# A hybrid attention block on one core: the FFN's gate and up products as seven block products from block 3 on, and p's projection ahead of the FFN

## Chip, core and metric

The kernel runs on one core of one Trainium2 chip. Such a core has five instruction streams that run beside each other and meet at semaphores: PE (TensorE, matrix products into the eight PSUM banks), DVE (VectorE, elementwise), ACT (ScalarE, activations and copies), POOL (GpSimd) and SP (SyncE, which here only issues transfers). Sixteen DMA engines move data between DRAM and the on-chip memory SBUF. The metric is the device time of one execution in microseconds (us).

## What is computed

One residual block on 512 tokens of width 1024, in float32. The attention part is left out here, since the change leaves its arithmetic as it is.

```python
def conv_ffn(h, w_gate, w_up, conv_w, conv_b, w_down):
    g = h @ w_gate                       # 1024 -> 2816
    gp = jnp.pad(g, ((0, 0), (2, 0), (0, 0)))
    conv = conv_b
    for j in range(3):                   # causal, along the tokens
        conv = conv + gp[:, j:j + s, :] * conv_w[j]
    return (jax.nn.silu(conv) * (h @ w_up)) @ w_down

x = x + concat[mla(h), diff(h)] @ w_out                  # h = rms_norm(x)
x = x + conv_ffn(rms_norm(x, ffn_norm_g), w_gate, w_up, conv_w, conv_b, w_down)
x = x + sigmoid(rms_norm(x, ple_norm_g) @ w_ple_gate) * (p @ w_ple_proj)
```

## The kernel before

Everything is kept transposed: x^T is eight blocks of 128 features by 512 tokens. A float32 product is made of three products of rounded parts: every operand is split into a rounded `hi` (ACT, a copy) and a remainder `lo` (DVE, a subtraction), and `mm3` (L151) issues hi·hi, hi·lo and lo·hi for each 128-row step of the contraction (L154, L155, L156). So a weight tile costs a load on SP's queue into one of three `raw` buffers (`load_w`, L142), an ACT copy (L147) and a DVE subtraction (L148) before PE may use it.

The FFN has 22 blocks of 128 hidden columns. For block f, `gu_full` (L782) makes the gate g and the up u, each 8 steps of the contraction times 3 matmuls of 128x128 by 512 tokens: 48 matmuls. `gu_post` (L768) then multiplies g by the tokens' norm factor r (`nr`; gr, DVE L772), runs the three-tap convolution (ACT L773, DVE L774 and L775), silu (ACT L776), r again (POOL L777), times u (DVE L778), and splits the result into `ah`, `al`. The norm factor is applied after the product, so that the products need only the unnormalised, split x (`h2h`, `h2l`, L191 and L192); r itself is made meanwhile, from one 512-column matmul with ones (L750).

The down projection goes in groups of 6, 6, 6 and 4 blocks: `down` (L794) makes for one of the eight blocks of x^T the sum over the group's blocks, and `add_x` (L575) adds it to x^T from PSUM. A further part, `ple` (L849), closes the kernel: for each block of x^T 24 matmuls for the gate `pg` and 6 for the projection of p (`pp`), then r (L862), sigmoid, times pp (L864), plus x (L865), and a store. It needs the squares of the final x^T summed over its blocks (L744, L745).

PE's order is the order of the code (`manual_schedule` is set for it alone); the order on the other engines is made by a scheduler when the program is built, and each engine, and each DMA queue, then works in that order strictly.

Of the kernel before, what the change touches and what calls it, by code (L numbers as in the profile page):

```python
# [20 lines left out]
P = 128  # L21
# [14 lines left out]
# columns of the packed per-partition array  # L36
# [15 lines left out]
DOWN_GROUPS = (6, 6, 6, 4)  # L52
# [3 lines left out]
# units of filling work at the attention's steps  # L56
# [7 lines left out]
# which of VectorE (0) and GpSimdE (1) does a step, by tiles  # L64
# [35 lines left out]
def hybrid_block(ctx: ExitStack, tc: tile.TileContext, a: dict, out: bass.AP):  # L100
# [4 lines left out]
    sb = ctx.enter_context(tc.tile_pool(name="sb", bufs=1))  # L105
    sm = ctx.enter_context(tc.tile_pool(name="sm", bufs=2))
    pp_ = ctx.enter_context(tc.tile_pool(name="ps", bufs=1, space=PS))
# [5 lines left out]
    def tt(name, dtype=F32):  # L113
        return sb.tile([P, T], dtype, tag="tt", bufs=16, name=name)

    def sq_tile(name):
        return sb.tile([P, D], F32, tag="sq", bufs=2, name=name)

    def pm_tile(name):
        return sb.tile([P, T], F32, tag="pm", bufs=PM, name=name)  # L120

    def pt_tile(name):
        return sb.tile([P, T], F32, tag="pt", bufs=2, name=name)

    def xn_tile(name):
        return sb.tile([P, D], F32, tag="xn", bufs=4, name=name)

    def kv_tile(name, dtype=F32):
        return sb.tile([P, NT, H, 160], dtype, tag="kv", name=name)

    def th_tile(name):
        return sb.tile([P, T], F32R, tag="th", bufs=8, name=name), sb.tile([P, T], F32R, tag="tl", bufs=8, name=name + "l")

    def small(name, shape):
        return sb.tile(shape, F32, name=name)

    def load_raw(src, n, name):
        raw = sb.tile([P, 1024], F32, tag="raw", bufs=3, name=f"raw_{name}")
# [3 lines left out]
    def load_w(src, n, name, eng=None):  # L142
        """a tile of weights as hi + lo"""
        raw = load_raw(src, n, name)
        hi = sb.tile([P, 1024], F32R, tag="hi", bufs=NW, name=f"hi_{name}")
        lo = sb.tile([P, 1024], F32R, tag="lo", bufs=NW, name=f"lo_{name}")
# [4 lines left out]
    def mm3(ps, blocks, first=True, last=True):  # L151
        n = len(blocks)
        for i, (xh, xl, wh, wl) in enumerate(blocks):
            TE.matmul(ps, xh, wh, start=first and i == 0, stop=False)  # L154
            TE.matmul(ps, xh, wl, start=False, stop=False)  # L155
            TE.matmul(ps, xl, wh, start=False, stop=last and i == n - 1)  # L156
# [28 lines left out]
    def split(h_, l_, src, col=None, eng=None):  # L185
        """hi and lo of src, times a gain for each partition"""
# [9 lines left out]
    # the tensor engine's clock and the activation tables get ready while the first loads run  # L196
    ones, warm = small("ones", [P, P]), small("warm", [P, 1])
# [11 lines left out]
    def squares(kq):  # L209
        """squares of x, for the sums over its columns"""  # L210
# [7 lines left out]
    cols = small("cols", [P, NCOL])  # L218
    nc.sync.dma_start(cols, a["cols"])
    xh, xl, wa = [], [], []  # L220
    for kq in range(4):
        raw = xn_tile(f"xT{kq}")
        xraw.append(raw)
        wr = sb.tile([P, 1024], F32, tag="raw", bufs=3, name=f"raw_a{kq}")
        wh, wl = (sb.tile([P, 1024], F32R, tag=i, bufs=NW, name=f"{i}_a{kq}") for i in ("hi", "lo"))
# [21 lines left out]
    ident = small("ident", [P, P])  # L247
# [20 lines left out]
    # latents: normalise  # L268
# [681 lines left out]
```

## Time and profile before

| | us |
|---|---|
| three runs | 702.42, 705.51, 705.87 |
| median | 705.51 |
| span of the profiled execution | 706.7 |
| attention and output projection, to the first FFN matmul | 265.8 |
| PE busy | 677.1 |
| DVE, ACT, POOL busy | 424.2, 288.4, 139.0 |

The span is that of one profiled execution, from the first to the last instruction; it stands 1.2 us above the median of the runs. PE's busy time counts a matmul from its issue to its modelled end, and matmuls overlap in the array, so the distance between two issues, not a matmul's duration, is what one costs. In a timeline row the numbers are start and duration, and in brackets the idle time before it with what ended it. In a row of a group, a count, the busy time, the mean duration in ns, and the idle time before with its releaser. In a row of DMA issues, the last number is the time from issue to landing.

### The profile page before, as it was taken

How to read it: one execution, taken by the hardware profiler on the slowest of the kernel's cores; microseconds unless marked ns; L12 is line 12 of the kernel's file. 1: busy time of each engine (PE TensorE's matmuls, PEld its weight loads, DVE VectorE, ACT ScalarE, POOL GpSimd, SP SyncE). 2: the span in 40 equal slices, each digit the busy share in tenths (PEclk: the TensorE clock that was granted, in tenths of full speed). 3: DMA queues.
4: the chain of work that ended last, by engine and by line, in shares of the span. 5: the costliest groups of instructions: out<-in, count | busy, mean ns of one | idle time of the engine just before them, and what ended most of it. 6: DMA issues, size and time to landing. Idle time of an engine off the chain costs nothing.

```text
span 706.7 us, 8596 instructions
## 1 busy us (share of the span) xinstructions
PE 677.1 (96%) x3242; PEld 554.8 (79%) x3242; DVE 424.2 (60%) x754; ACT 288.4 (41%) x500; POOL 139.0 (20%) x136
## 2 busy tenths in 40 slices
PE   7988889999999997999999999999999999999997
PEld 6877678788878785788888888888888888877886
DVE  6689964634779878774544545534554455468743
ACT  6156645536666654343421333312333233255210
POOL 6458341504010125021100011100101000132000
PEclk9899999999999998999999999999999999999999
DMA  7332014303311103233213333222233132243101
GB/s 261 106 121 89 30 60 135 120 1 111 129 30 61 31 31 105 74 99 110 90 42 108 119 102 106 90 90 89 90 103 103 63 119 90 89 150 104 60 31 45
DMA packets 19552, 63.38 MB, mean 90 GB/s; under 512 B 2220, under 2 KB 2988, under 8 KB 19384
## 3 DMA queue, kind: packets, MB, share of 16 engines
q1 hardware_dynamic: 18776, 60.25, 25.9%
q0 software_dynamic: 448, 2.37, 1.1%
q8 instruction: 25, 0.41, 0.2%
q10 hardware_dynamic: 288, 0.23, 0.1%
q14 instruction: 15, 0.12, 0.1%
HBM read 60.73 MB, written 3.42 MB: 91 GB/s over the span
## 4 chain that ended last, share of the span: by engine, by line
PE 76%; DVE 14%; ACT 3%; issue 2%; POOL 2%; DMA 2%; SPq 0%; ACTq 0%; DVEq 0%; POOLq 0%
PE u L154 6%; PE u L156 6%; PE u L155 6%; PE g L156 6%; PE g L155 6%; PE g L154 6%; PE dn L154 5%; PE dn L155 5%; PE dn L156 5%; PE pg L154 2%; PE pg L156 2%; PE pg L155 2%; PE mo L527 2%; PE zd L154 2%; PE zd L156 2%
## 5 line engine op out<-in xcount | busy, mean ns | idle before, releaser
L777 POOL TENSOR_TENSOR cv<-cv,nr 128x512 f32<-128x512 f32 x22 | 28.7, 1308 | 297.9 <-ACT cv L776 297.9
L155 PE MATMUL g<-h2l,hi_g 128*128 128x512 f32 x176 | 69.6, 396 | 4.7 <-DVE h2l L192 4.7
L154 PE MATMUL dn<-ah,hi_dn 128*128 128x512 f32 x176 | 69.8, 397 | 2.1 <-DVE x L575 2.1
L154 PE MATMUL u<-h2h,hi_u 128*128 128x512 f32 x176 | 70.5, 401 | 0.0
L154 PE MATMUL g<-h2h,hi_g 128*128 128x512 f32 x176 | 70.4, 400 | 0.0
L156 PE MATMUL u<-h2h,lo_u 128*128 128x512 f32 x176 | 70.2, 399 | 0.0
L156 PE MATMUL g<-h2h,lo_g 128*128 128x512 f32 x176 | 70.0, 398 | 0.0
L155 PE MATMUL u<-h2l,hi_u 128*128 128x512 f32 x176 | 69.6, 396 | 0.0
L156 PE MATMUL dn<-ah,lo_dn 128*128 128x512 f32 x176 | 69.5, 395 | 0.0
L575 DVE TENSOR_TENSOR x<-x,dn 128x512 f32<-128x512 f32 x32 | 21.9, 685 | 51.1 <-PE dn L156 51.1
L147 ACT CAST hi_dn<-raw_dn 128x1024 fp32r<-128x1024 f32 x22 | 23.1, 1051 | 69.3 <-PE dn L155 29.7
L772 DVE TENSOR_TENSOR gr<-g,nr 128x512 f32<-128x512 f32 x22 | 15.1, 691 | 53.7 <-PE g L156 53.6
L147 ACT CAST hi_g<-raw_g 128x1024 fp32r<-128x1024 f32 x22 | 23.0, 1047 | 57.9 <-PE dn L155 39.9
L147 ACT CAST hi_u<-raw_u 128x1024 fp32r<-128x1024 f32 x22 | 23.1, 1052 | 55.4 <-PE g L155 50.0
L155 PEld LDWEIGHTS g<-h2l,hi_g 128*128 128x128 f32 x176 | 33.3, 189 | 13.9 <-DVE h2l L192 5.9
L778 DVE TENSOR_TENSOR cv<-cv,u 128x512 f32<-128x512 f32 x22 | 15.1, 688 | 44.4 <-POOL cv L777 44.4
L154 PEld LDWEIGHTS dn<-ah,hi_dn 128*128 128x128 f32 x176 | 33.0, 187 | 10.8 <-DVE x L575 1.9
L154 PE MATMUL zd<-hi_d,xh 128*128 128x512 f32 x96 | 40.2, 418 | 0.0
L156 PEld LDWEIGHTS u<-h2h,lo_u 128*128 128x128 f32 x176 | 33.5, 190 | 8.4
L155 PEld LDWEIGHTS u<-h2l,hi_u 128*128 128x128 f32 x176 | 33.5, 190 | 8.2
L156 PEld LDWEIGHTS g<-h2h,lo_g 128*128 128x128 f32 x176 | 33.3, 189 | 8.1
L154 PEld LDWEIGHTS u<-h2h,hi_u 128*128 128x128 f32 x176 | 33.6, 191 | 7.7
(371 smaller groups left out, 1657.4 us busy)
## 6 DMA issues: line engine op xcount, KB each, us to landing
raw_g<-in_w_gate SPq DMA_DIRECT2D x22, 512.0 KB, 3.6
raw_u<-in_w_up SPq DMA_DIRECT2D x22, 512.0 KB, 3.5
raw_dn<-in_w_down SPq DMA_DIRECT2D x22, 512.0 KB, 3.5
raw_d<-in_w_d SPq DMA_DIRECT2D x12, 512.0 KB, 3.7
raw_o<-in_w_out SPq DMA_DIRECT2D x8, 512.0 KB, 4.0
raw_pg<-in_w_pg SPq DMA_DIRECT2D x8, 512.0 KB, 3.6
x<-in_xT SPq DMA_DIRECT2D x4, 512.0 KB, 5.6
out<-ot SPq DMA_DIRECT2D x7, 256.0 KB, 2.0
```

The lines of the kernel that those rows point to most:

```text
L147: S.copy(hi[:, :n], raw[:, :n])
L154: TE.matmul(ps, xh, wh, start=first and i == 0, stop=False)
L155: TE.matmul(ps, xh, wl, start=False, stop=False)
L156: TE.matmul(ps, xl, wh, start=False, stop=last and i == n - 1)
L527: TE.matmul(po[:, w], pt[:, tsl[j]], kv[j][:, h, 96:], start=j == 0, stop=j == t)
L575: V.tensor_tensor(xb(b), xb(b), ps, op=ALU.add)
L772: V.tensor_tensor(gr, pg_, nrm["r"], op=ALU.mult)
L777: G.tensor_tensor(cv, cv, nrm["r"], op=ALU.mult)
L778: V.tensor_tensor(cv, cv, pu, op=ALU.mult)
```

## The change

**The FFN's products.** From block 3 on (`NPLAIN = 3`), g and u of a block are not two separate products. With the contraction cut into two halves (rows k 0 to 3 and k 4 to 7), the tokens into two halves of 256 columns, and gate and up as the two column blocks of one 2x2 block matrix, a 2x2 by 2x2 block product is made with seven block products and sums (Winograd's form of Strassen's scheme). Each product is 4 steps times 3 matmuls of 256 token columns: 84 matmuls of 256 columns in place of 48 of 512. Products share PSUM: ACT copies a partial sum from one bank to another (L892, L897, L903), and later products are added on top of it (`again`). The seven are named `11`, `12`, `S2`, `S4`, `S3`, `S1` and `22`; two blocks are interleaved on PE: S2(f), 11(f+1), S4(f), S3(f), 12(f+1), S1(f), a down unit, 22(f), a down unit.

**Sums of weights.** One array `w_gu` holds gate and up of a block (1,280 KB with the second copy of a part). An accumulating DMA of 512 KB on POOL's queue (L824) adds gate parts to up parts in SBUF, after the load; two DVE additions (L827, L828) make the other sums `s24`; then four splits follow for each block (`wA`, `wT`, `wS` of 1024 columns, `w22` of 512), of which only `wA` and the raw tile have two buffers.

**Sums of tokens.** The FFN's input is normalised ahead (`tokens`, then `token_sums` for the sums), so r is needed before the first FFN matmul, and gu_post no longer multiplies by r. r itself is now made from four one-column matmuls, a reciprocal square root on 128x4 values, a diagonal matrix `dg` and one matmul `nrb` that spreads it over the partitions.

**The rest.** The projection of p is made ahead of the FFN (`pp_unit`), stored to DRAM (`pps`) and read back in the tail. The down groups are 4, 4, 4, 4, 4 and 2, as units that are called up one at a time. SBUF pools are released and taken anew between stages.

```diff
-DOWN_GROUPS = (6, 6, 6, 4)
+DOWN_GROUPS = (4, 4, 4, 4, 4, 2)
+NPLAIN = 3
...
+    def pp_unit(b):
+        ps, w = bank("acc", f"pp{b}"), wpp[b // 4]
+        mm3(ps, [(w[0][:, c[k]], w[1][:, c[k]], ptw[0][:, k * T:k * T + T], ptw[1][:, k * T:k * T + T]) for k in range(2)])
+        o = pm_tile("ppo")
+        S.copy(o, ps)
+        nc.sync.dma_start(pps[b], o)
...
+    for i, b in enumerate(order):
+        square(i, b)
+    for b in range(NK):
+        pp_unit(b)
+        if b == 1:
+            norm_r()
+        if b == 3:
+            norm_b()
...
+    def raw5(f, n):
+        raw = ffn.tile([P, 2560], F32, tag="raw5", bufs=2, name=f"gu{f}")
+        nc.sync.dma_start(raw[:, :n], a["w_gu"][f][:, :n])
+        return raw
+
+    raws = {0: raw5(0, 2048), 1: raw5(1, 2048)}
...
+    def w_prep(f):
+        raw = raws.pop(f)
+        q = [raw[:, 512 * i:512 * i + 512] for i in range(5)]
+        nc.gpsimd.dma_start(raw[:, 1536:].rearrange("p (i c) -> p i c", i=2), a["w_gu"][f][:, :2048].rearrange("p (i c) -> p i c", i=2)[:, :, :512], accum_op=ALU.add)
+        s24 = ffn.tile([P, 1024], F32, tag="s24", name=f"s24_{f}")
+        wa_ = hl(raw[:, :1024], "wA", f, bufs=2)
+        V.tensor_tensor(s24[:, :512], q[0], q[4], op=ALU.add)
+        V.tensor_tensor(s24[:, 512:], q[1], s24[:, :512], op=ALU.add)
+        wt_ = hl(s24, "wT", f)
+        ws_ = hl(raw[:, 1536:], "wS", f)
+        w2_ = hl(q[2], "w22", f, 512)
+        if f + 2 < NF:
+            raws[f + 2] = raw5(f + 2, 2560)
...
+    def gu_units(f, w):
+        x, g = bank("acc", f"gx{f}")[:, :H2], bank("tp", f"g{f}")
+        product(x, w["11"], tb["11"])
+        S.copy(g[:, t1], x)
+        yield
+        product(g[:, t1], w["12"], tb["21"], True)
+        yield
+        product(x, w["S2"], tb[2], True)
+        S.copy(g[:, t2], x)
+        yield
+        product(g[:, t2], w["S4"], tb["22"], True)
+        yield
+        u = bank("ob", f"u{f}")
+        product(x, w["S3"], tb[3], True)
+        S.copy(u[:, t1], x)
+        yield
+        y = bank("lg", f"gy{f}")[:, :H2]
+        product(y, w["S1"], tb[1])
+        ys = ffn.tile([P, H2], F32, tag="y", name=f"y{f}")
+        S.copy(ys, y)
+        V.tensor_tensor(g[:, t2], g[:, t2], ys, op=ALU.add)
+        V.tensor_tensor(u[:, t2], x, ys, op=ALU.add)
+        yield
+        product(u[:, t1], w["22"], tb[4], True)
+        gu_post(f, g, u, -1.0)
+        yield
...
-        V.tensor_tensor(gr, pg_, nrm["r"], op=ALU.mult)
-        S.activation(cv, gr, AF.Identity, bias=cols[:, C_CB + f:C_CB + f + 1], scale=cw[2])
+        S.activation(cv, g, AF.Identity, bias=cols[:, C_CB + f:C_CB + f + 1], scale=cw[2])
...
-        G.tensor_tensor(cv, cv, nrm["r"], op=ALU.mult)
-        V.tensor_tensor(cv, cv, pu, op=ALU.mult)
+        V.scalar_tensor_tensor(cv, u, sign, cv, op0=ALU.mult, op1=ALU.mult)
...
+    for f in range(NPLAIN, NF):
+        if f + 1 < NF:
+            W[f + 1] = w_prep(f + 1)
+            g1 = gu_units(f + 1, W[f + 1])
+        next(g)
+        if g1:
+            next(g1)
+        next(g)
+        next(g)
+        if g1:
+            next(g1)
+        next(g)
+        pump()
+        next(g)
+        pump()
+        g = g1
```

**Three places in the order of the instructions.** First DVE in the middle of the FFN. Before, for blocks 9 to 12 (`gr` and `cv` belong to gu_post of one block, `lo_g` and `lo_u` are the weights of the block two or three further on):

```order
L772 TENSOR_TENSOR gr_3811<-g9_3761,nr_2928 128x512
L148 TENSOR_TENSOR lo_u11_3908<-raw_u11_3905,hi_u11_3907 128x1024
L774 SCALAR_TENSOR_TENSOR cv_3812<-gr_3811,cols_89,cv_3812 128x511
L775 SCALAR_TENSOR_TENSOR cv_3812<-gr_3811,cols_89,cv_3812 128x510
L778 TENSOR_TENSOR cv_3812<-cv_3812,u9_3762 128x512
L148 TENSOR_TENSOR lo_g12_3977<-raw_g12_3974,hi_g12_3976 128x1024
```

Now, for block 10 on PE, with what each row waits for; `gx10` is the bank x of `gu_units(10)`, `y10` its S1 product, and DMASW is POOL's queue:

```order
L195 TENSOR_TENSOR wTl11_4420<-s24_11_4412,wTh11_4419 128x1024 [waits PE_49,Activation_49]
L195 TENSOR_TENSOR wAl12_4581<-gu12_4276,wAh12_4580 128x1024 [waits DMAHW2_49,Activation_49]
L827 TENSOR_TENSOR s24_12_4579<-gu12_4276 128x512 [waits DMASW4_49,DVE_49]
L828 TENSOR_TENSOR s24_12_4579<-gu12_4276,s24_12_4579 128x512 [waits DVE_49]
L195 TENSOR_TENSOR wSl11_4424<-gu11_4109,wSh11_4423 128x1024 [waits PE_49,Activation_49]
L909 TENSOR_TENSOR g10_4292<-g10_4292,y10_4512 128x256 [waits Activation_49]
L910 TENSOR_TENSOR u10_4473<-gx10_4291,y10_4512 128x256
L581 TENSOR_TENSOR x2_1859<-x2_1859,dn44_4528 128x512 [waits PE_49]
L921 SCALAR_TENSOR_TENSOR cv_4554<-g10_4292,cols_95,cv_4554 128x511 [waits Activation_49]
L922 SCALAR_TENSOR_TENSOR cv_4554<-g10_4292,cols_95,cv_4554 128x510 [waits DVE_49]
L195 TENSOR_TENSOR w22l11_4428<-gu11_4109,w22h11_4427 128x512 [waits PE_49,Activation_49]
```

The sums for block 12, which wait for the accumulating DMA of block 12, now stand ahead of the last weights of block 11 and of the two additions that finish block 10.

Second, SP's queue around the start of the FFN. Before, after the last weights of the output projection:

```order
L139 DMA raw_o13_2720<-in_w_out 128x1024
L139 DMA raw_g0_2864<-in_w_gate 128x1024
L139 DMA raw_u0_2870<-in_w_up 128x1024
L139 DMA raw_g1_2953<-in_w_gate 128x1024
L139 DMA raw_u1_2959<-in_w_up 128x1024
```

Now:

```order
L145 DMA raw_o13_2726<-in_w_out 128x1024
L145 DMA raw_pT_2732<-in_pT 128x1024
L145 DMA raw_pp0_2801<-in_w_pp 128x1024
L145 DMA raw_pp1_2827<-in_w_pp 128x1024
L753 DMA pps_2847<-ppo_2879 128x512
L753 DMA pps_2847<-ppo_2889 128x512
...
L753 DMA pps_2847<-ppo_2962 128x512
L753 DMA pps_2847<-ppo_2972 128x512
L803 DMA gu0_2983<-in_w_gu 128x2048
L803 DMA gu1_2985<-in_w_gu 128x2048
```

The first FFN weights now stand behind the eight stores of p's projection (four of them left out here).

Third, DVE in the tail, at the last down group. Before (`dn18` is the last group, of four blocks, `lo_pg` weights of the last part, `h3l` the split of the finished x^T):

```order
L148 TENSOR_TENSOR lo_dn1811_5224<-raw_dn1811_5221,hi_dn1811_5223 128x1024
L575 TENSOR_TENSOR x3_1855<-x3_1855,dn127_5096 128x512
L575 TENSOR_TENSOR x0_1849<-x0_1849,dn180_5140 128x512
L192 SCALAR_TENSOR_TENSOR h3l_5127<-x0_1849,cols_89,h3h_5126 128x512
L575 TENSOR_TENSOR x0_1849<-x0_1849,dn181_5158 128x512
L148 TENSOR_TENSOR lo_pg00_5326<-raw_pg00_5323,hi_pg00_5325 128x1024
L192 SCALAR_TENSOR_TENSOR h3l_5127<-x0_1849,cols_89,h3h_5126 128x512
L575 TENSOR_TENSOR x1_1851<-x1_1851,dn182_5177 128x512
```

Now (`dn20` is the last group, of two blocks):

```order
L195 TENSOR_TENSOR lo_pg10_6371<-raw_pg10_6368,hi_pg10_6370 128x1024
L581 TENSOR_TENSOR x3_1861<-x3_1861,dn166_6330 128x512
L195 TENSOR_TENSOR lo_pg20_6377<-raw_pg20_6374,hi_pg20_6376 128x1024
L581 TENSOR_TENSOR x3_1861<-x3_1861,dn167_6344 128x512
L195 TENSOR_TENSOR lo_pg30_6383<-raw_pg30_6380,hi_pg30_6382 128x1024
L154 TENSOR_TENSOR lo_dn2000_6394<-raw_dn2000_6391,hi_dn2000_6393 128x1024
L154 TENSOR_TENSOR lo_dn2010_6450<-raw_dn2010_6447,hi_dn2010_6449 128x1024
L581 TENSOR_TENSOR x0_1855<-x0_1855,dn200_6397 128x512
L581 TENSOR_TENSOR x0_1855<-x0_1855,dn201_6408 128x512
L195 TENSOR_TENSOR lo_pg01_6668<-raw_pg01_6665,hi_pg01_6667 128x1024
L198 SCALAR_TENSOR_TENSOR h3l_6387<-x0_1855,cols_95,h3h_6386 128x512 x2
```

The last group's weights now come behind weights of the last part, and a group's product on PE is half as long beside the same DVE work for each block of x^T.

More of the change, by code (lines that the diff above doesn't have):

```diff
@@ L744, in norm_in @@
             S.activation(sq, xb(b), AF.Square)
-            (G if b % 2 else V).tensor_tensor(nrm["ss"], nrm["ss"], sq, op=ALU.add)
+            V.tensor_tensor(nrm["ss"], nrm["ss"], sq, op=ALU.add)
     def norm_r():
-        ps = bank("ob", "nr")
-        TE.matmul(ps, ones, nrm["ss"], start=True, stop=True)
-        r, m, g, t = (w_[:, i] for w_ in [sb.tile([P, DH, T], F32, tag="strip", name="nr")] for i in range(4))
-        rms(r, ps, T, D, m, (g, t))
-        return r
-    h2h = sb.tile([P, NK, T], F32R, tag="st", name="h2h")
@@ L757, in hybrid_block @@
[L757 to L770 removed]
+        ss, ps = nrm["ss"], bank("ob", "nr")
@@ new lines, in product @@
+    def product(ps, w, b, more=False):
+        mm3(ps, [(w[0][:, tsl_k[k]], w[1][:, tsl_k[k]], b[0][:, k], b[1][:, k]) for k in range(K2)], not more, True, more)
+    def gu_units(f, w):
[24 more added lines that the diff above has]
+        yield
@@ L831, in hybrid_block @@
-    h3h = sb.tile([P, NK, T], F32R, tag="st", name="h3h")
-    h3l = kv_tile("h3l", F32R).rearrange("p t h d -> p (t h d)")[:, :NK * T].rearrange("p (k t) -> p k t", t=T)
+    for k in range(NK):
+        tokens(k % K2, k // K2)
+    W[1] = w_plain(1)
+    for k in range(K2):
+        token_sums(k)
+    for f in range(NPLAIN):
+        if f:
+            W[f + 1] = w_plain(f + 1) if f + 1 < NPLAIN else w_prep(f + 1)
+        plain(f, W[f])
+    g = gu_units(NPLAIN, W[NPLAIN])
+    next(g)
+    next(g)
```

288 lines of the change are left out of this document (181 added, 107 removed).

## The prediction

> **What bounds the kernel now.** I read the page's busy times and its chain of waits first, then the windows of the FFN, then single matmuls in the timeline.
>
> ```profile
> PE 677.1 (96%) x3242; PEld 554.8 (79%) x3242; DVE 424.2 (60%) x754; ACT 288.4 (41%) x500; POOL 139.0 (20%) x136
> PE 76%; DVE 14%; ACT 3%; issue 2%; POOL 2%; DMA 2%; SPq 0%; ACTq 0%; DVEq 0%; POOLq 0%
> 300.00:400.00 100.00, 100.00 (x431) 80.64 (x430) 50.79 (x62) 33.06 (x41) 10.61 (x8) 1.00 0.31 95
> 692.97 0.40 PE L156 MATMUL pg<-h3h,lo_pg 128*128 128x512 f32 x1
> 693.20 0.39 PE L154 MATMUL pg<-h3h,hi_pg 128*128 128x512 f32 x1
> 695.28 0.28 PE L154 MATMUL pg<-h3h,hi_pg 128*128 128x256 f32 x1
> ...
> 697.88 0.28 PE L155 MATMUL pg<-h3l,hi_pg 128*128 128x256 f32 x1
> 698.00 0.28 PE L156 MATMUL pg<-h3h,lo_pg 128*128 128x256 f32 x1
> ```
>
> The window row (length, then PE, PEld, DVE, ACT, POOL busy, granted clock, DMA share, GB/s) shows that the FFN is bound by PE alone: busy for all of 100 us at full clock, with DVE at half. 431 matmuls in 100 us are 0.232 us for one of 512 columns, and the first pair of timeline rows has that distance. The three rows after them are the first and the last of 24 matmuls of 256 columns: (698.00 - 695.28) / 23 = 0.118 us for one. A block costs 48 matmuls for gate and up and, spread out, 24 of the down projection: 72 x 0.232 = 16.7 us. So fewer columns on PE do pay, for as long as nothing else takes more than a block's PE time.
>
> **The change, part by part.**
>
> *Products.* In 19 blocks 48 x 0.232 = 11.14 us become 84 x 0.118 = 9.91: 1.23 us each, **-23.5 us** in all. p's projection is 48 matmuls in either place (11.1 us): 0. PE's own time for a block is then 9.9 + 24 x 0.232 = 15.5 us.
>
> *Entry of the FFN.* Before:
>
> ```profile
> 265.76 0.40 PE L154 MATMUL g<-h2h,hi_g 128*128 128x512 f32 x1
> 272.49 0.51 PE L155 MATMUL g<-h2l,hi_g 128*128 128x512 f32 x1 [2.85 <-DVE h2l L192]
> 275.27 0.80 PE L155 MATMUL g<-h2l,hi_g 128*128 128x512 f32 x1 [1.82 <-DVE h2l L192]
> 276.29 0.63 PE L154 MATMUL g<-h2h,hi_g 128*128 128x512 f32 x1
> 276.71 0.63 PE L155 MATMUL g<-h2l,hi_g 128*128 128x512 f32 x1
> 284.91 0.59 PE L750 MATMUL nr<-ss,ones 128*128 128x512 f32 x1
> 274.00:278.00 4.00, 2.73 (x7) 2.03 (x8) 4.00 (x4) 1.86 (x3) 2.32 (x2) 0.57 0.34 131
> L744 ACT ACTIVATE nsq<-x 128x512 f32<-128x512 f32 x7 | 4.3, 615 | 0.0
> L745 DVE TENSOR_TENSOR ss<-ss,nsq 128x512 f32<-128x512 f32 x3 | 2.1, 686 | 0.0
> L188 ACT CAST ah<-cv 128x512 fp32r<-128x512 f32 x22 | 13.7, 621 | 2.4 <-DVE cv L778 2.4
> 250.01 0.17 DVE L161 TENSOR_SCALAR ro<-mo 128x4 int32<-128x4 int32 x1
> ...
> 250.61 0.16 DVE L173 SCALAR_TENSOR_TENSOR ro<-rs_t,ro 128x4 f32<-128x4 f32 x1
> 250.69 0.15 DVE L175 SCALAR_TENSOR_TENSOR rs_g<-rs_t,rs_g 128x4 f32<-128x4 f32 x1
> ...
> 251.55 0.16 DVE L173 SCALAR_TENSOR_TENSOR ro<-rs_t,ro 128x4 f32<-128x4 f32 x1
> raw_g<-in_w_gate SPq DMA_DIRECT2D x22, 512.0 KB, 3.6
> L659 SPq DMA_DIRECT2D x<-in_xT x4: 378/438/510, 171.8 to 173.3; - x4
> DMA to landing us min/median/max: 4.4/5.6/7.2
> 107.43 0.77 POOL L546 DMA_DIRECT2D vec<-vb  x1 [0.30 <-POOL vb L545]
> 109.81 0.58 POOL L547 DMA_DIRECT2D vec<-vec  x1 [1.61 <-DMA vec<-vb]
> vec<-vb POOLq DMA_DIRECT2D x1, 10.0 KB, 2.1
> L147 ACT CAST hi_dn<-raw_dn 128x1024 fp32r<-128x1024 f32 x22 | 23.1, 1051 | 69.3 <-PE dn L155 29.7
> 278.62 1.21 DVE L148 TENSOR_TENSOR lo_u<-raw_u,hi_u 128x1024 fp32r<-128x1024 f32 x1
> ```
>
> Block 0's 48 matmuls ran from 265.76 to 284.91, 19.15 us for 11.14 us of work: 8.0 lost, to waits for h2l and, after them, to a clock of 0.57 (matmuls 0.42 apart). The change has p's projection to fill the first wait, but puts r ahead of everything. The sum of squares has six blocks still to go when PE is done with the output projection: 0.69 + 0.62 + 6 x 0.69 = 5.4 us, against two units of p (2.8): 3 lost. The square root on 128x4 values takes 251.71 - 250.01 = 1.7; with the diagonal (0.69), four small matmuls, the spreading one (0.59 to its end) and some 1.9 for hand-overs and the mean, an estimate, 4.9 us against the next two units' 2.8: 2 lost. Then the second place of the order: gu0's load stands on SP behind the eighth store, which waits for the copy after the last unit. From there a copy (0.62), an issue (0.33) and a load of 1,024 KB. Four loads of 512 KB issued together landed, first to last, (173.3 + 7.2 - 171.8 - 4.4) / 3 = 1.43 us apart, so the load takes 3.5 + 1.43 = 4.95; 0.3 to wake the waiter (issue 107.43, landing 2.1 later, the next instruction at 109.81), hi 1.05, lo 1.2: 8.3 us idle. The stalls bring the half clock back, 13 matmuls x 0.2 = 2.6, and more for three stalls than for two: 4. Together 17.5 against 8.0: **+9.5 us**, between 6 (no clock loss) and 14 (r's steps as slow as the DVE operations beside POOL, below).
>
> *The loop.* The first place of the order closes a ring: the load of gu(f+2) needs the buffer that w22l(f) reads last, and w22 has one buffer, which PE's 22(f-1) must have read. The accumulating DMA waits for that load; s24(f+2) waits for it on DVE; behind s24(f+2) in DVE's order stand wSl(f+1) and the two additions of block f; 22(f) on PE needs the second of them; w22l(f+1) needs 22(f); and the load of gu(f+3) needs w22l(f+1). Once round is one block. Its parts:
>
> ```profile
> L575 DVE TENSOR_TENSOR x<-x,dn 128x512 f32<-128x512 f32 x32 | 21.9, 685 | 51.1 <-PE dn L156 51.1
> L148 DVE TENSOR_TENSOR lo_dn<-raw_dn,hi_dn 128x1024 fp32r<-128x1024 f32 x22 | 27.7, 1261 | 7.0 <-ACT hi_dn L147 6.0
> 698.32 0.42 DVE L862 TENSOR_TENSOR sg<-pg,nr 128x256 f32<-128x256 f32 x1 [1.35 <-PE pg L156]
> strip<-vec POOLq DMA_DIRECT2D x1, 1024.0 KB, 5.4
> 276.40 2.29 DVE L148 TENSOR_TENSOR lo_g<-raw_g,hi_g 128x1024 fp32r<-128x1024 f32 x1
> ```
>
> DVE: two sums of 512 columns (0.69 each), wSl (1.26), two additions of 256 (0.42 each): 3.5. PE: 22, 12 x 0.118 and 0.16 to the end of the last, 1.57. Then w22's hi on ACT 0.62 and lo on DVE 0.69. That is 6.4, and five hand-overs between engines about 0.9. The load of 1,280 KB: 3.5 + 1.5 x 1.43 = 5.65. The accumulating DMA of 512 KB is not in the trace. Below: as a plain one on POOL's queue, 2.1 + (5.4 - 2.1) / 2 = 3.75. Above: its bytes moved twice, as it reads what it writes, 5.4 like the 1,024 KB of strip. I take 4.7, nearer the upper, since every element is read, added and written back. Round: 6.4 + 0.9 + 5.65 + 4.7 = **17.65 us**, from 16.7 to 18.35, where PE needs 15.5. Nothing covers the rest: POOL and SP have no work queued that could start earlier, and PE's next unit is behind 22(f).
>
> By the Trainium skill ("DMA: Bandwidth & Descriptors", section "Anatomy of one DMA — SWDGE (gpsimd) path"), a transfer takes about 2.0 us plus its bytes at 436 GB/s, which gives 3.2 for the 512 KB and 5.0 for the load; the ring would then be 15.5, no longer than PE. The strip row speaks against it: by that fit it would be 4.4, and it took 5.4.
>
> In 14 steady blocks that is 14 x 2.15 = 30 us; laid out from the entry, block 3 (no down units yet to cover anything) loses 5.5, the next two 3, the last ones 1.2: **+40 us**, from 24.5 to 51 with the bounds of the accumulate. Of this some 10 us would stay even with instant transfers: after S1, PE's cover is one down unit (2.8), while hi and lo of wS and the two additions take 3.2, 0.4 in each block, and the start-up remains.
>
> *Tail.* The third place. The last group has two blocks, six matmuls for each block of x^T (1.4 us) where there were twelve (2.8), beside the same DVE work:
>
> ```profile
> L192 DVE SCALAR_TENSOR_TENSOR h3l<-x,cols,h3h 128x512 fp32r<-128x512 f32 x8 | 7.0, 880 | 5.9 <-ACT h3h L191 5.9
> 263.94 0.74 DVE L192 SCALAR_TENSOR_TENSOR h2l<-x,cols,h2h 128x512 fp32r<-128x512 f32 x1
> L148 DVE TENSOR_TENSOR lo_pg<-raw_pg,hi_pg 128x1024 fp32r<-128x1024 f32 x8 | 12.3, 1536 | 1.2 <-ACT hi_pg L147 1.1
> ```
>
> dn2000 is the fifth weight load through three raw buffers, loaded and split behind four of pg: PE waits about 3.2, and 0.9 for the last weights of the group ahead. Then DVE has eight additions (5.5), eight h3l (5.9 undisturbed at 0.74), seven sums of squares (4.8), the lo of dn2010 and of four pg tiles (6.3): 22 us, while PE has the group's 11.1 and a first unit of pg, 5.6, before it needs the last h3l, 16.7. 5.1 more: **+9.5 us** with 0.3 of hand-overs, between 4 (the DVE work that isn't needed for h3l slips back) and 12.
>
> *Small parts.* gu_post loses gr on DVE and the product on POOL, both off PE's path. The normalised tokens and their sums, about 40 us of DVE and ACT over the first blocks, lie beside plain blocks of 11.1 us; their weights are early, so I count 0 for them, and 3 if they are late.
>
> **Sum**: 706.7 - 23.5 + 9.5 + 40 + 9.5 = 742.2, less the 1.2 by which the profiled span exceeds the median of the runs: 741. Forecast **740 us**; with the bounds of its parts 725 to 754.
>
> **Rivals.**
> (a) *The accumulate and the load land so early that the ring is below PE's time.* The loop then keeps the 10 us of start-up and 0.4 per block: 742.2 - 30 - 1.2 = **711**. For it: the DMA share is only 0.31, so nothing competes. Against it: 6.4 us of the ring are durations of this trace, and a plain load of 512 KB alone takes 3.6, of which the ring has one longer and one that is also added.
> (b) *The other side: PE alone paces the kernel.* Without POOL's work beside it DVE is quicker (lo 1.21 alone, 2.29 beside POOL), consecutive DVE operations overlap by some 0.08 at their ends, and if the two hand-overs of the ring fall below 15.5 as well, the loop's waits vanish (1 left) and the tail's shrink to 4: 706.7 - 23.5 + 9.5 + 1 + 4 - 1.2 = **697**. It decides from a ring under 15.5, that is 2.15 us less than my parts; entry must still be paid.
> (c) *The accumulate is slower than its bytes twice*, or PE's idle spells in the loop lower the clock as the 1.8 and 2.9 us did at the entry (0.57). Each us in the ring is 14 + 1.5 = 15.5 us; landing in 6.5 instead of 4.7, the time is 741 + 28 = **769**. For it: 2.1 us waits come in every block, close to the 1.82 that left the clock low. By the Trainium skill ("TensorE: Matmul & The Clock Gate", section "Part 1: The HAM clock gate (the "warmup" mystery)") the clock falls for want of work in a whole window of a few us; no spell here is that long in my sum, and the row at 276.29 stands behind two spells, so I leave it out of the sum.
>
> **How the numbers follow.** Forecast 0.50, (a) 0.17, (b) 0.18, (c) 0.15. A measurement of this kernel tells 0.5%, 3.5 us, from no change. Faster by that (under 702): (b) and 0.02 of (a), 0.20. Within it: 0.05 of (a) and a few of (b)'s upper side: 0.07. Slower: 0.73. The range leaves out half of (b) and two thirds of (c), 0.19: 697 to 766; the likeliest case's own is 725 to 754.
>
> **What would show it.** In the loop's windows: PE's matmuls at 0.118 and 0.232, 108 of them in 17.7 us and not 15.5; the row of 22 waiting about 2 us on DVE's L910 in each block, and L827 waiting for POOL's DMA; the accumulate 4.7 us from issue to landing, the load of gu 5.7. At the entry an idle of some 8 us before the first g matmul, released by DVE's lo of gu0; in the tail, idle before L154 of dn20 and of pg. Wrong is the sum if L827 finds its transfer landed (then 711 or less), if PE idles in a block elsewhere than before 22, or if the clock in the loop is under 0.95. Each term is read by itself: products, entry, loop, tail.

## The result: slower by a tenth, 772 us

| | before | after |
|---|---|---|
| median, us (6 runs each) | 705.01 (702.42 to 706.62) | 772.19 (770.21 to 778.44) |
| span of the profiled execution, us | 706.7 | 776.6 |

The ratio is 1.0975, with a 95% interval from 1.0932 to 1.1018. The profiled execution of the changed kernel was the longest of its six, about 6 us above their median, so the sums below are made against its span of 776.6.

The page of the changed kernel, against the lines shown of before: busy times, granted clock, the chain of waits, and the issues of the block's weights.

```profile
PE 684.1 (88%) x3936; PEld 594.8 (77%) x3936; DVE 493.0 (63%) x909; ACT 348.6 (45%) x629; POOL 104.7 (13%) x117
PEclk8899999999999988989999998999899999999999
PE 36%; DMA 29%; DVE 23%; issue 6%; ACT 4%; POOL 2%; SPq 0%; POOLq 0%; DVEq 0%; ACTq 0%
DMA gu<-in_w_gu 27%; DVE wSl L195 3%; PE u L160 2%; PE pg L160 2%; PE mo L533 2%; PE pg L162 2%; PE pg L161 2%; PE zd L160 2%; PE zd L162 2%; PE zd L161 2%; DVE s L827 2%; PE u L161 2%; DVE w22l L195 2%; PE o L160 1%; PE o L161 1%
gu<-in_w_gu SPq DMA_DIRECT2D x19, 1280.0 KB, 5.6
gu<-in_w_gu POOLq DMA_DIRECT2D x19, 512.0 KB, 6.0
```

PE's busy time even rose, since a matmul's modelled end overlaps the next and there are more of them; the chain tells more. PE had 76% of it and has 36%; DMA had 2% and has 29%, nearly all of it the two transfers of a block's weights. In the wait table of the same execution (who waited for whom, us in total, times, longest) one row holds most of PE's idle time in the FFN:

```profile
PE u L160 <- DVE u L910: 49.9, 18, 6.6
PE g L160 <- ACT wAh L194: 7.4, 1, 7.4
PE dn L160 <- DVE x L581: 3.6, 2, 1.8
PE dn L160 <- ACT hi_dn L153: 3.3, 1, 3.3
PE nr L768 <- DVE ss L762: 3.0, 1, 3.0
```

The first row is the product 22 of each block waiting for the addition u = x + y on DVE. The others are the entry (`wAh` of block 0, `nr`) and the tail (`x`, `hi_dn`). How a block goes round shows in the timeline, here from block 12's 22 to block 13's; the bracket gives the idle time before the row and what ended it:

```profile
516.64 0.69 DVE L827 TENSOR_TENSOR s<-gu 128x512 f32<-128x512 f32 x1 [4.14 <-DMA gu<-in_w_gu]
519.45 0.42 DVE L910 TENSOR_TENSOR u<-gx,y 128x256 f32<-128x256 f32 x1
520.02 0.36 PE L160 MATMUL u<-bth,w22h 128*128 128x256 f32 x1 [3.82 <-DVE u L910]
520.93 0.41 PE L160 MATMUL u<-bth,w22h 128*128 128x256 f32 x1
521.99 0.41 PE L162 MATMUL u<-bth,w22l 128*128 128x256 f32 x1
522.29 0.62 ACT L194 CAST w22h<-gu 128x512 fp32r<-128x512 f32 x1 [1.94 <-PE u L161]
522.94 0.69 DVE L195 TENSOR_TENSOR w22l<-gu,w22h 128x512 fp32r<-128x512 f32 x1 [1.02 <-ACT w22h L194]
523.66 0.33 SPq L803 DMA_DIRECT2D gu<-in_w_gu  x1
529.85 1.20 POOL L824 DMA_DIRECT2D gu<-in_w_gu  x1 [18.82 <-DMA gu<-in_w_gu]
535.97 0.69 DVE L827 TENSOR_TENSOR s<-gu 128x512 f32<-128x512 f32 x1 [2.31 <-DMA gu<-in_w_gu]
539.35 0.35 PE L160 MATMUL u<-bth,w22h 128*128 128x256 f32 x1 [1.99 <-DVE u L910]
```

This is the ring of the prediction, whose links release one another in this order: the sums of weights on DVE, the additions, 22 on PE, the split of the next w22, the next load, the accumulating transfer, the next sums. From L827 to L827 it takes 535.97 - 516.64 = 19.33 us. Over the steady part, 14 rounds from 380.44 to 656.07, the mean is 19.69:

```profile
380.44 0.35 PE L160 MATMUL u<-bth,w22h 128*128 128x256 f32 x1 [3.49 <-DVE u L910]
656.07 0.36 PE L160 MATMUL u<-bth,w22h 128*128 128x256 f32 x1 [2.73 <-DVE u L910]
```

### The profile page after: what moved, and what is told of

Read it like the earlier page. It is cut to its first block, busy times and chain, and to the rows that moved or that the text cites. A ratio compares the mean times of both kernels' runs of the same rounds, so it can differ in the third digit from the quotient of the medians.

```text
span 776.6 us, 10308 instructions
## 1 busy us (share of the span) xinstructions
PE 684.1 (88%) x3936; PEld 594.8 (77%) x3936; DVE 493.0 (63%) x909; ACT 348.6 (45%) x629; POOL 104.7 (13%) x117
## 4 chain that ended last, share of the span: by engine, by line
PE 36%; DMA 29%; DVE 23%; issue 6%; ACT 4%; POOL 2%; SPq 0%; POOLq 0%; DVEq 0%; ACTq 0%
DMA gu<-in_w_gu 27%; DVE wSl L195 3%; PE u L160 2%; PE pg L160 2%; PE mo L533 2%; PE pg L162 2%; PE pg L161 2%; PE zd L160 2%; PE zd L162 2%; PE zd L161 2%; DVE s L827 2%; PE u L161 2%; DVE w22l L195 2%; PE o L160 1%; PE o L161 1%
## 5 line engine op out<-in xcount | busy, mean ns | idle before, releaser
L824 POOL DMA_DIRECT2D gu<-in_w_gu x19 | 22.7, 1194 | 420.4 <-DMA gu<-in_w_gu 304.3
L161 PE MATMUL dn<-al,hi_dn 128*128 128x512 f32 x176 | 73.4, 417 | 0.0
L160 PE MATMUL u<-bth,w22h 128*128 128x256 f32 x76 | 27.2, 358 | 49.9 <-DVE u L910 49.9
L195 DVE TENSOR_TENSOR wTl<-s,wTh 128x1024 fp32r<-128x1024 f32 x19 | 23.3, 1225 | 56.2 <-ACT wTh L194 56.2
L827 DVE TENSOR_TENSOR s<-gu 128x512 f32<-128x512 f32 x19 | 13.2, 692 | 54.3 <-DMA gu<-in_w_gu 52.0
L162 PEld LDWEIGHTS dn<-ah,lo_dn 128*128 128x128 f32 x176 | 35.9, 204 | 10.5 <-DVE lo_dn L154 2.4
L161 PEld LDWEIGHTS dn<-al,hi_dn 128*128 128x128 f32 x176 | 36.5, 207 | 6.6
L161 PE MATMUL zd<-lo_d,xh 128*128 128x512 f32 x96 | 38.3, 399 | 0.0
L521 DVE TENSOR_REDUCE nm<-ml 128x1 f32<-128x128 f32 (+3 forms) x32 | 15.6, 488 | 31.0 <-PE ml L519 31.0
L154 DVE TENSOR_TENSOR lo_dn<-raw_dn,hi_dn 128x1024 fp32r<-128x1024 f32 x22 | 26.8, 1222 | 7.2 <-ACT hi_dn L153 7.2
L195 DVE TENSOR_TENSOR wAl<-gu,wAh 128x1024 fp32r<-128x1024 f32 x22 | 26.8, 1219 | 2.7 <-ACT wAh L194 2.7
L195 DVE TENSOR_TENSOR wSl<-gu,wSh 128x1024 fp32r<-128x1024 f32 x21 | 25.6, 1218 | 3.1 <-ACT wSh L194 3.1
L194 ACT CAST wAh<-gu 128x1024 fp32r<-128x1024 f32 x22 | 23.0, 1044 | 8.9 <-PE g L161 4.5
```

The source lines that it names most:

```text
L154: (eng or V).tensor_tensor(lo[:, :n], raw[:, :n], _f32(hi[:, :n]), op=ALU.subtract)
L160: TE.matmul(ps, xh, wh, start=first and i == 0, stop=False, skip_group_check=again)
L161: TE.matmul(ps, xh, wl, start=False, stop=False, skip_group_check=again)
L162: TE.matmul(ps, xl, wh, start=False, stop=last and i == n - 1, skip_group_check=again)
L194: S.copy(h_, src)
L195: (eng or V).tensor_tensor(l_, src, _f32(h_), op=ALU.subtract)
```

## Experiments

Each shows its edit against the kernel it was built on; unless said otherwise that is the changed kernel. The times of 1 to 7 are of one run each; the kernel before took 706.82 us beside 1 to 4, 708.35 beside 5, and from 702.0 to 708.5 in nine runs beside 6 to 9, so a difference of 4 or 5 us between two single runs is not told by the time alone.

**1. A second buffer for w22.**

```diff
-        w2_ = hl(q[2], "w22", f, 512)
+        w2_ = hl(q[2], "w22", f, 512, 2)
-    t5 = lambda name: ffn.tile([P, T], F32, tag="t5", bufs=3, name=name)
+    t5 = lambda name: ffn.tile([P, T], F32, tag="t5", bufs=1, name=name)
```

> Two buffers for w22 in place of one (and one for cv in place of three, which makes the room). Theory, the ring: the load of gu(f+2) no longer waits for PE's 22 of the block before, only for wSl, and the ring shrinks from the 19.7 us measured between two starts of 22 (DVE 3.4, PE 2.3, ACT and DVE 1.4, load 6.2, accumulate 6.1) to DVE 2.5 + load 6.2 + accumulate 6.1 = 14.8, below PE's 15.5. Blocks then come every 15.5 to 16.5 us, the granted clock in the loop rises above 0.97, and the time falls from 772 by 14 x 3.2 to 14 x 4.2, to 713 to 727. Rival, PE is slowed in the loop by something else than the ring (PSUM traffic of ACT and DVE, or DVE's amount of work): blocks still come every 18 us or more, time above 750.

Measured 730.77 us, 41 less than the changed kernel and 4 above the range. The loop does nearly what was expected, with both transfers still in it: the windows below give 16.6 us for a block (15.5 to 16.5 expected), and the clock is back at 1.00. Some rounds still wait up to 2.8 us for L910. The rival falls.

**2. The same bytes copied, not added.**

```diff
-        nc.gpsimd.dma_start(raw[:, 1536:]..., accum_op=ALU.add)
+        nc.gpsimd.dma_start(raw[:, 1536:]...)
```

> The transfer on POOL's queue copies its 512 KB in place of adding them (the sums of gate and up parts are left out, so the weights are not those of the scheme). Theory, adding costs because every byte is also read back: landing falls from 6.0 us to the 3.75 us that the plain transfers of the kernel before bound it by, the ring from 19.7 to about 17.5, time 772 - 31 = 741 (735 to 748). Rival, the price is that of the software queue (1.2 us of POOL for each issue, descriptors of 2 KB) and not of the adding: landing stays above 5.3 and the time above 760.

Measured 740.23 us. The transfer landed after 4.1 us in place of 6.0 and the round took 17.4 us in place of 19.7. The rival, a landing that stays above 5.3 us, falls. What the edit took away cost 1.9 us for 512 KB, and the ring hands that on to every block. It is not the adding alone, though: without the addition the same bytes also go in half as many packets, as the queue's rows show (packets, MB, share of the 16 engines' span; changed kernel, then copied):

```profile
q0 software_dynamic: 5616, 12.33, 9.2%
q0 software_dynamic: 3184, 12.33, 5.7%
```

A block's transfer is 256 pieces of 2,048 bytes when it adds and 128 of 4,096 bytes when it copies. In the trace of the changed kernel a piece of 2,048 bytes that adds takes 178 ns on its DMA engine (median), a plain one of that size, on SP's queue, 84 ns, and a plain one of 4,096 bytes 159 ns. So two plain small pieces cost about what one large one does, and most of the time on the DMA engines goes to the adding. The issue also kept POOL for 1.19 us in place of 0.72. No run varied the size of the pieces alone.

**3. The sums on DVE.**

```diff
-        nc.gpsimd.dma_start(raw[:, 1536:]..., accum_op=ALU.add)
+        V.tensor_tensor(q[3], q[3], q[0], op=ALU.add)
+        V.tensor_tensor(q[4], q[4], q[2], op=ALU.add)
```

> The same sums by two DVE additions of 512 columns in the raw tile in place of the accumulating transfer. Theory, the ring: 6.1 us go and 1.3 come, 19.7 - 4.8 = 14.9, below PE's 15.5; blocks every 15.5 to 16.5 us, time 713 to 730. DVE's work of a block rises to about 13 us of these 15.5. Rival, DVE becomes the bound: it works in order on some 17 pieces for each block with ACT's copies ahead of them, blocks come every 17 us or more, time above 738.

Measured 721.62 us. 19 transfers are exchanged for 38 DVE instructions, and it is faster by 51 us: DVE is busy for 154 of 200 us in the loop, and PE waits for its addition 0.3 us in most blocks.

**4. All blocks plain.**

```diff
-NPLAIN = 3
+NPLAIN = 22
...
+        pump()
+        pump()
```

> All 22 blocks plain (48 matmuls of 512 columns, no sums of weights, no accumulating transfer), all else as in the changed kernel: normalised input, p's projection ahead of the FFN, down groups of 4, units of the down projection called after each block. Theory: against the kernel before only the entry (measured: first FFN matmul at 291.8 in place of 265.8, with 11.1 of p's projection in it, and 1.5 more at the low clock; 16.4 against 8.0, +8.4) and the tail (about +10 to 15) are left, 705 + 8.4 + 12 = 725 (718 to 733); so seven products, as built, cost 40 to 55 us although they save 23.5 on PE. Rival, the surroundings carry much of the loss (smaller down groups, fewer weight buffers): above 740.

Measured 715.49 us, 2.5 below the range. So the surroundings (entry, tail, smaller groups) cost 9 us net against the 706.82 beside it, and seven products as built cost a further 57. The 9 us hide something that nobody had planned. The stretch from 400 to 600 us of this kernel, and then of the kernel before (columns as in the prediction's window row):

```profile
400.00:600.00 200.00, 200.00 (x881) 165.04 (x880) 91.48 (x113) 60.27 (x75) 0.00 (x0) 1.00 0.27 90
400.00:600.00 200.00, 200.00 (x861) 161.32 (x860) 96.26 (x115) 63.87 (x76) 16.82 (x13) 1.00 0.30 95
```

PE is busy throughout in both, at full clock and with matmuls of 512 columns alone, but one costs 0.227 us here and 0.232 before. Over 22 blocks of 72 matmuls that is some 8 us, so entry and tail lose more than the 9 that are left. Why the matmuls stand closer together no run shows.

**5. Half of the accumulating transfer, out of the ring.** The half that s24 needs is added on DVE; the other half stays on POOL's queue, and now only wS needs it, a block later.

```diff
-        nc.gpsimd.dma_start(raw[:, 1536:]..., accum_op=ALU.add)
+        nc.gpsimd.dma_start(q[3], a["w_gu"][f][:, :512], accum_op=ALU.add)
+        V.tensor_tensor(q[4], q[4], q[2], op=ALU.add)
```

> The changed kernel with half of the accumulating transfer (256 KB, the sum that only wS needs) and the other half (the sum that s24 needs) as one DVE addition. s24 then no longer waits for POOL's queue, and the transfer has until wSl of the block, a block later. Theory: what costs is the place of the transfer in the ring, not the transfer; the ring is 19.7 - 6.1 + 0.7 = 14.3, blocks come every 16.1 us as with DVE sums, time 719 to 726. On the price: if adding costs by the byte, 256 KB land after 2.1 + (6.0 - 2.1) / 2 = 4.05 us; if it is a fixed surcharge of 1.9 on the plain transfer, after about 5.0. Rival: accumulating transfers hold up the other transfers or the engines wherever they stand: blocks every 17.5 us or more, time above 740.

Measured 720.90 us, as with DVE sums. An accumulating transfer for each of the 19 blocks costs nothing that these runs show once no block's end depends on it. It landed after 4.3 us, nearer the price by the byte than the fixed surcharge.

Stretch 400 to 600 us of these kernels. Columns: length, busy time and count of PE, PEld, DVE, ACT, POOL, then granted clock, DMA share, GB/s. In order: changed kernel,

```profile
400.00:600.00 200.00, 170.70 (x1092) 156.62 (x1093) 116.77 (x156) 78.93 (x121) 11.92 (x10) 0.93 0.43 119
```

second buffer for w22,

```profile
400.00:600.00 200.00, 190.15 (x1300) 174.21 (x1299) 137.16 (x181) 94.52 (x144) 14.56 (x13) 1.00 0.51 143
```

copied and not added,

```profile
400.00:600.00 200.00, 184.08 (x1242) 168.79 (x1241) 128.86 (x170) 90.49 (x138) 8.67 (x12) 0.98 0.40 136
```

sums on DVE,

```profile
400.00:600.00 200.00, 193.88 (x1331) 178.35 (x1330) 154.25 (x210) 96.33 (x148) 0.00 (x0) 1.00 0.31 111
```

and half the transfer out of the ring:

```profile
400.00:600.00 200.00, 195.29 (x1340) 179.58 (x1339) 148.71 (x199) 96.93 (x149) 11.03 (x13) 1.00 0.44 128
```

A block is 108 matmuls, so 200 x 108 / count is the time of a block: 19.8, 16.6, 17.4, 16.2 and 16.1 us. The second buffer alone raises the DMA share from 0.43 to 0.51 and takes 3 us off a block, so bandwidth was not what was short.

**6 and 7. Entry and tail, each on the kernel with DVE sums.** Entry: the stores of p's projection leave SP's queue, r is used from PSUM and made two units later, and the lo of the first weights moves to GpSimd.

```diff
-        nc.sync.dma_start(pps[b], o)
+        nc.scalar.dma_start(pps[b], o)
-        if b == 1:
+        if b == 3:
             norm_r()
-        if b == 3:
+        if b == 5:
             norm_b()
...
-    S.copy(nrm["r"], nrm.pop("b"))
+    nrm["r"] = nrm.pop("b")
...
+        e = G if f < 2 else V
```

> On top of the kernel with DVE sums (721.6): the stores of p's projection on ACT's queue in place of SP's, so that gu0 and gu1 load while PE makes p's projection; r used from PSUM without a copy; the matmuls for r two units later, where they cover each other; the lo of the first two blocks' weights on GpSimd. Theory, the entry's wait is the load behind the stores and the chain of r: the first FFN matmul starts at 284 to 286 in place of 290.6, the wait before it falls from 7.9 to under 5, time 714 to 717. Rival, the tokens (eight times 1.4 us on DVE after r) set the start whatever is done with the load: no gain above 2 us, time 719 or more.

Measured 717.53 us, just above the theory's 714 to 717 and short of the rival's 719. The first FFN matmul starts at 282.96, but the attention ended 1.7 us earlier in this execution, so the gain is about 6 us there; then two matmuls wait for GpSimd's lo:

```profile
282.96 0.79 PE L160 MATMUL g<-b1h,wAh 128*128 128x512 f32 x1 [5.24 <-ACT wAh L194]
285.72 0.80 PE L162 MATMUL g<-b1h,wAl 128*128 128x512 f32 x1 [1.54 <-POOL wAl L195]
288.23 0.79 PE L162 MATMUL u<-b1h,wSl 128*128 128x512 f32 x1 [0.86 <-POOL wSl L195]
```

Tail: groups of 2, 4, 4, 4, 4, 4 (with the first group's units in blocks 3 to 5), and the last group's weights loaded ahead of the last part's.

```diff
-DOWN_GROUPS = (4, 4, 4, 4, 4, 2)
+DOWN_GROUPS = (2, 4, 4, 4, 4, 4)
...
-    pg_w = ple_w(0)
...
         ws = down_w(f0, nf, dh)
+        if dh == 1:
+            pg_w = ple_w(0)
```

> On top of the kernel with DVE sums (721.6): down groups 2, 4, 4, 4, 4, 4 in place of 4, 4, 4, 4, 4, 2, with the first group's units in blocks 3 to 5, and the last group's weights loaded ahead of the last part's. Theory, the tail's 13 us of loss (measured: waits 3.5, 1.8 and some smaller, the rest low clock behind them) come from weights that queue behind others in three raw buffers and from units of 1.4 us beside unchanged DVE work: 9 of the 13 go, and 2 of the waits of block 3, time 708 to 713. Rival, DVE's 22 us of work after the last group set the tail: less than 4 go, time above 717.

Measured 716.89 us, 4.7 less where about 11 were expected, and just under the rival's 717. The waits for x are gone, but the one for hi_dn stayed at 3.5 us. The split of the second half's weights has only the two buffers that the first half's matmuls read until 646 us, and it stands on ACT behind work on x^T, so that it starts at 648.96; which of the two holds it longer was not tried.

**8 and 9. Both together, on DVE sums and on all plain.**

> DVE sums, the entry and the tail together. Theory, the terms add: 721.6 - 6 - 11 = 704.5 (700 to 709), about the time of the kernel before. Rival, they hide behind one another (the entry's gain is lost to weights that come late, or the like): 711 or more.

Measured 714.00 us (ratio to before 1.0118, interval 1.0008 to 1.0228); the terms did not add, and the rival's 711 or more was met. The two traces show which term fell short. From the last matmul of the output projection to the first of the FFN there are 25.9 us with DVE sums alone (264.75 to 290.63) and 20.0 with both (266.34 to 286.30), so the entry gave the 6 us that were expected of it. From the last gate or up matmul to the end there are 87.3 us (632.49 to 719.8) and 83.7 (629.06 to 712.8), so the tail gave 3.6 of 11. The FFN between them took 0.9 longer, and the attention of the second execution ended 1.6 later.

> The entry and the tail on top of the kernel with all blocks plain (715.5). Theory, the same two terms come off, less in the first blocks where nothing waits: 715.5 - 5 - 9 = 701.5 (697 to 706), so that seven products without the ring are worth no more than plain blocks (they save 19 x 1.1 on PE, and give 19 x 0.5 and some 7 at their start back). Rival, seven products win once the rest is mended: this kernel is slower than the one with DVE sums, entry and tail by 3 us or more.

Measured 707.22 us (1.0045, interval 1.0013 to 1.0076), 1.2 above the theory's range. Plain blocks were the better choice at this point: with the ring gone, seven products still waited 10.9 us for DVE's addition and lost time at their start.

**10 and 11. Both down units between S1 and 22, with the second buffer for w22 of experiment 1, and the last weights all loaded at once, on the kernel with both; and the last weights alone with plain blocks.**

```diff
         next(g)
-        pump(2 if f in (3, 4) else 1)
-        next(g)
-        pump()
+        pump(3 if f in (3, 4) else 2)
+        next(g)
...
+    wp.update(pool=ple_, rawpool=ple_, raw=4, w=8)
+    wlast = [down_w(f0, nf, dh) for dh in range(2)]
+    pg_w = ple_w(0)
```

> On top of DVE sums, entry and tail (714.0): both down units of a block stand between S1 and 22 on PE (before, one ahead of 22 and one behind), with two buffers for w22 (room from one for cv), and the last group's weights go to the room that the FFN left, all four loaded at once ahead of the last part's. Theory: in the kernel with all three the 19 starts of 22 waited 10.9 us in all for DVE's L911, since one down unit (2.8) covers S1's copy, the hi and lo of wS and two additions (3.2) not quite; two units (5.6) cover them, blocks come every 15.6 us in place of 16.1 to 17.2, 10 us go; the tail gives 3 more. Time 701 (697 to 706), faster than the kernel before by some 0.5%. Rival: 22 starts later and so does everything that waits for it (w22, the next load), the ring grows to 17 us and the time stays at 712 or above.

> All blocks plain, with the same entry and the same last weights as the kernel with covered 22 (707.2 before the latter). Theory: the tail gives 2 to 3, time 705 (702 to 708), so that seven products, with every wait mended that was found, gain 3 to 6 us over plain blocks of the same build. Rival, the two come out within 2 us of each other: what PE saves in columns is given back in the first blocks and in the sums.

Measured 704.02 us for the first (ratio to before 0.9974, interval 0.9941 to 1.0006) and 706.51 for the second (1.0032, 1.0001 to 1.0063), both within their ranges. The wait for the addition is gone from the middle of the FFN, as the wait rows of the kernel with both (first) and with covered 22 (second) show, in the stretch from 340 to 620 us; a block takes 15.7 us:

```profile
PE u L160 <- DVE u L911: 10.9, 18, 2.5
```

```profile
PE g L160 <- ACT g L898: 3.0, 6, 1.2
PE u L160 <- DVE u L911: 0.3, 1, 0.3
400.00:600.00 200.00, 197.40 (x1375) 184.71 (x1374) 156.39 (x211) 99.73 (x152) 0.00 (x0) 1.00 0.31 108
```

So with what was found mended, seven products come out faster than plain blocks of the same build, by 2.5 us between the medians of ten runs each and by 4.3 between the means (95% interval 1.8 to 6.8), where 3 to 6 were expected. They cannot be told from the kernel before. No version tried is shown to beat it.

## Why the prediction was wrong

The forecast was 740 us with a range from 697 to 766. The sign and the mechanism, the ring, held; the size of the loop's term did not. The terms, against the profiled span, came out like this:

| term | predicted, us | measured, us |
|---|---|---|
| products | -23.5 | -20.5 |
| entry | +9.5 | about +8 |
| loop | +40 | about +71 |
| tail | +9.5 | about +13 |

The measured terms come to 71.5 us, the two spans differ by 69.9. Two things stand in no row: some 4 us less for the matmuls of 512 columns that are left, which stand closer together as in experiment 4, and 1 us more because the attention ended later in this execution. With them the account closes to within 2 us. Two sums of the prediction do not come out quite as written: the entry's parts give 17.3 and not 17.5, and the loop's lower end 25.3 (40 less 0.95 x 15.5) and not 24.5. Neither matters for the result.

**Loop.** This is the term that failed, and in it the price of the accumulating transfer. The prediction bounded it by 3.75 and 5.4 us and called the upper end "its bytes moved twice"; it landed after 6.0, outside both bounds, and the next instruction on DVE started 6.12 after the issue. At the prediction's own price of 15.5 us for each us of the ring, the 1.3 us above its 4.7 are 20 of the 31 us by which the loop came out longer. The plain neighbour that bounded it from below was too low as well: copied, the transfer landed after 4.1 us and not 3.75 (experiment 2). The load took 5.6 as predicted (5.65), but with SP's issue and POOL's start 6.19. The product 22 took 2.27 to the next split in place of 1.57, since it ran in part at half clock. The other parts fell within 0.3 us: 3.38 to the start of 22, 1.37 for the split. These lengths have the hand-overs in them, which the prediction counted apart as 0.9. Together 3.38 + 2.27 + 1.37 + 6.19 + 6.12 = 19.33 where 17.65 was written, and 14 steady blocks at 19.69 and not 15.6 cost 57 us and not 30. The rest, some 14, is the start-up: from the first of the seven products at 326.46 to 380.44 there are 54.0 us for 39.8 of PE's work. The 22 of blocks 3, 4 and 5 waited 6.6, 0.6 and 3.5 of these, and slow matmuls behind the waits make up most of the rest, where 8.5 was written.

That the ring was the cause is shown by taking it apart in four ways: a second buffer, a shorter transfer, no transfer, and a transfer that no block's end waits for. In all four the time of a block came within 0.1 us of what the ring's lengths let expect, and the kernel's time within 4 us of the range given for it. With no transfer in the ring, and with half of it out, most starts of 22 are 16.09 us apart, where PE's work is 15.6: close to the 0.4 for each block that the prediction expected to stay.

**The clock.** The prediction named it under rival (c), left it out of the sum, and gave a clock under 0.95 in the loop as a sign of being wrong. Its row in the loop is 0.93, and the rows of 22 show when: after the wait of 3.82 us the matmuls stand 0.21 apart in place of 0.12 from the fifth on (520.93 to 521.99 above, five intervals), after 1.99 they stay at full speed. Shorter waits do it too:

```profile
421.56 0.47 PE L160 MATMUL u<-bth,w22h 128*128 128x256 f32 x1 [2.81 <-DVE u L910]
422.04 0.41 PE L162 MATMUL u<-bth,w22l 128*128 128x256 f32 x1
423.96 0.41 PE L162 MATMUL u<-bth,w22l 128*128 128x256 f32 x1
```

The last two rows are nine intervals apart, 0.213 each. Of the 15 starts of 22 from 380.44 to 656.07, the ten with a wait from 2.73 to 4.42 us were all followed by matmuls 0.21 apart, and the five with 1.05 to 1.99 by none. By the Trainium skill ("TensorE: Matmul & The Clock Gate", section "Part 1: The HAM clock gate (the "warmup" mystery)") the clock falls after an idle window of about 3.4 us. The trace agrees with this only in part: waits of 2.73, 2.81, 2.81 and 3.16 us, all shorter, lowered it as well. The spells that were 2.15 in the sum became 2.7 to 4.4 in ten rounds of 15, and this is how a clock came in that the prediction had left out. Most of the lost clock was hidden in PE's waits; on the ring it is the 0.7 of the product 22 in the round shown, about 0.6 in the mean of the 15.

**Rival (c)** gave 769 for a transfer that lands in 6.5 us or a lowered clock. Both halves of it happened, each in part: the landing at 6.0 and the clock at 0.93. That 769 lies so near to 772 is partly luck, since its 28 us were meant for the landing alone. Rival (a), a ring below PE's time, and rival (b), PE as the pace, fall: L910 ended 18 of PE's waits.

**Products.** Seven eighths of the saving is there: 72 matmuls of 256 columns from 525.84 to 534.46 are 0.1197 us each and not 0.118, so a block saves 11.14 - 10.06 = 1.08 us. The failing was not that 24 matmuls are few: those of 256 columns at the end of the changed kernel are 0.120 apart too. A matmul's price is not the same in the two builds, in either length (0.118 and 0.120 for 256 columns, 0.232 and 0.227 for 512, the latter in experiment 4). Against plain blocks of its own build seven products save 48 x 0.227 - 10.06 = 0.84 us a block, 16 us in all, which is what experiments 8 to 11 had to win.

**Entry.** Right in its parts and about right in the sum:

```profile
268.90 16.54 SPq L753 DMA_DIRECT2D pps<-ppo  x8
272.56 1.05 PE L768 MATMUL nr<-ones,ss 128*128 128x1 f32 x8 [2.96 <-DVE ss L762]
285.53 0.88 SPq L803 DMA_DIRECT2D gu<-in_w_gu  x2
290.70 1.04 ACT L194 CAST wAh<-gu 128x1024 fp32r<-128x1024 f32 x1 [2.36 <-DMA gu<-in_w_gu]
291.79 0.80 PE L160 MATMUL g<-b1h,wAh 128*128 128x512 f32 x1 [7.37 <-ACT wAh L194]
```

The wait for the sum of squares was 2.96 (3 written), the load of gu0 stood behind the eight stores and PE idled 7.4 (8.3 written). From the end of the output projection at 266.7 to 291.8 there are 25.1 us, 11.1 of them p's projection; that leaves 14.0, and the first eight matmuls lost 2.0 more (3.81 us from 291.79 to 295.60 for 1.85 of work): 16.0 where 17.5 was written, against 8.0 before.

**Tail.** The waits for weights that it named are there (hi_dn 3.3, lo_dn 1.1). The 5.1 us before the last part, for DVE's split of the last x^T, did not come: DVE's work showed as two waits of 1.8 for x ahead of the last group's products. After these waits the clock is low, which the sum did not carry: from 656.07 PE had 99.4 us of work and 5.2 of ending, 760.7, and the kernel ended at 776.6. That is 16 us lost; the kernel before lost about 3 in its tail (two waits of 2.1 us together and about 1 of low clock), so the change is +13.

```profile
706.89 0.50 PE L160 MATMUL dn<-ah,hi_dn 128*128 128x512 f32 x1 [3.26 <-ACT hi_dn L153]
716.83 0.47 PE L160 MATMUL dn<-ah,hi_dn 128*128 128x512 f32 x1 [1.79 <-DVE x L581]
721.60 0.50 PE L160 MATMUL dn<-ah,hi_dn 128*128 128x512 f32 x1 [1.78 <-DVE x L581]
```

Of the 16 us, 8.7 are waits that stand on PE's rows, and the rest is in matmuls that stand further apart than at full clock. No run of its own took the two apart.

## What to carry to other kernels

When a change takes work off the engine that is the bound, list the rings that it closes: follow each new transfer from its buffer's last reader through the instructions that wait for it, in the order of each engine, until the buffer is met again; one single-buffered pair of tiles, 4 KB a partition, turned two transfers into the pace of the kernel. An error in a part of a ring is paid once for every round, so the part that no trace shows needs the widest bound, not the middle of two neighbours. And a saving of 7% on the bound engine's work in a stage is only worth having when what is put around it (sums, splits, copies) has cover at every step: here mending it all gave back what was lost and no more than that could be told.

## What the runs showed of the hardware that was not expected

- A transfer on POOL's queue that adds: 512 KB in pieces of 2,048 bytes land after 6.0 us, 256 KB after 4.3; the same 512 KB without adding, in pieces of 4,096 bytes, after 4.1. The first two points give, as an estimate, 2.6 us and 1.7 for each 256 KB.
- A piece of 2,048 bytes that adds keeps its DMA engine for 178 ns, a plain one of that size for 84.
- The issue keeps POOL for 1.19 us with 512 KB and 0.85 with 256 KB that add, and for 0.72 with the 512 KB that do not.
- Two sums of 512 columns on DVE (0.69 us each) replace it for less than a quarter of its time.
- Waits of PE of 2.73 to 3.16 us, four of them, brought half the clock behind them; waits of 1.05 to 1.99, five of them, did not.
